# A slot table in DRAM in place of one-hot matmuls, and small tiles on 128 rows, in a routed expert layer

## The chip, the cores and the metric

The kernel runs on one core of one Trainium2 chip. The metric is the device time of one execution in microseconds (us). The median of three runs of the kernel before is 2848.63 us (2845.64 to 2850.64).

## The reference, cut to what matters

One encoder layer works on 1024 tokens of 1024 channels. After a mixing part (Fourier branch, attention, projections) comes a routed expert part, and that is what the change touches:

```
logits = u @ w_router + b_router                 # 1024 x 32
top_vals, top_idx = top_k(logits, 4)
top_w = softmax(top_vals)
for each expert e, for the tokens that chose it:
    h = u[tokens] @ w_gate_up[e] + b_gate_up[e]  # 1024 -> 2048
    gate = min(h[:, :1024], 7);  up = clip(h[:, 1024:], -7, 7)
    act = (up + 1) * gate * sigmoid(1.702 * gate)
    y = act @ w_down[e] + b_down[e]              # 1024 -> 1024
    out[tokens] += y * top_w
```

All of it is in 32-bit floats. Each product of matrices is made of three products of rounded halves (`hi` and `lo`), so each weight must be split on the chip into `whi` and `wlo` before TensorE may use it.

## The kernel before

**Routing.** The tokens go in eight tiles of 128. For tile `i`, `logits(i)` finds the four chosen experts, and `place(i)` counts with two small matmuls (L878, L879) which slot of each expert a token gets, and computes the weights (L889). The weights are cut into three bf16 parts (L897 to L900) and, with the slot numbers, transposed (L904) into `ct`. `accumulate(i)` multiplies `ct` with the expert biases `b_down` and adds the result to the output rows `acc_d` by an accumulating DMA on GpSimd's queue (L924, L926). At the end `in_order` (L932) turns slot numbers and weights into the order of the ranked experts (`posR`, `RH`). The experts are ranked by load after tile 6 (`ranking`); from there on rank 0 is the fullest.

**The expert stage.** Ranks 0 to 13 hold more than 128 slots and form lane a; ranks 14 to 31 hold 128 or 64 and form lane b. `plan` (from `moe_plan`) interleaves the two lanes step by step. An expert has twelve chunks of weights of 1 MB, so there are 384 chunks: steps 0 to 7 for gate and up, 8 to 11 for down; lane b has two more steps that transpose the activations (`at`, L1204). SyncE (SP) issues the loads of the chunks in the order of the plan, from three buffers `wraw` (`pew`, bufs=3). Per chunk ScalarE makes `whi` (L144) and VectorE `wlo` (L145); the chunk's buffer is free when both have read it.

**Tokens of an expert.** They are handled in 51 blocks of up to 128 slots, 33 in lane a and 18 in lane b. For a block, `one_hot` compares slot numbers with an iota on VectorE (L1080), eight bf16 matmuls with the one-hot tile (L1088) yield six numbers per slot, they are copied (`q6`, L1090), and `slot_info` makes from them the token for the gather (`gi`), the row for the scatter (`si`) and the weight (`wt`) in six short VectorE instructions (L997 to L1003). GpSimd gathers the rows of `u2_d` by an indirect DMA into `xya` or `xyb` (L1007); TensorE transposes them (L1103). In lane b, `rows` starts each pair of chunks with a matmul of the tile `sel` and the biases `b2`, both on 64 partitions (L1179), followed by the weights' own matmuls (L1183, L1184). `weigh` multiplies the result by `wt` (L1226 to L1230), and GpSimd adds it to `acc_d` by an indirect DMA, the scatter (L1011), once the fourth chunk of down is done. The next expert of a lane is fetched while the present one is at its chunks of gate and up.

A loop for experts that overflow their slots follows (from L1347); it has no rounds with this input.

Of the kernel before, what the change touches and what calls it, by code (L numbers as in the profile page):

```python
# [23 lines left out]
P = 128  # L24
# [6 lines left out]
NB_MAX = 64  # L31
ALPHA = 2.0 ** 0.25
# [63 lines left out]
def f32(ap):  # L96
    return ap.bitcast(F32)
# [7 lines left out]
def layer_kernel(ctx, tc, x, c, w_ada, b_ada, w_in, q_norm_g, k_norm_g, w_fourier, w_attn_o, w_out,  # L105
                 ln1_g, ln1_b, w_router, b_router, w_gate_up, b_gate_up, w_down, b_down,
                 ln2_g, ln2_b, t_cd, t_seq, t_rope, t_cap, t_idx, out):
# [5 lines left out]
    RS = "right"  # L113
# [104 lines left out]
    pyt = fo.enter_context(tc.tile_pool(name="pyt", bufs=1, side=RS))  # L218
# [3 lines left out]
    pfw = fws.enter_context(tc.tile_pool(name="pfw", bufs=1, side=RS))  # L222
# [29 lines left out]
    with tc.tile_pool(name="px", bufs=1) as px, tc.tile_pool(name="pada", bufs=3) as pada:  # L252
# [12 lines left out]
        act.dma_start(acc_d[S:S + P, :], x[0:P, :])  # L265
        xs = px.tile([P, NX, D], F32, name="xs")
# [70 lines left out]
    with tc.tile_pool(name="pfc", bufs=1) as pfc, tc.tile_pool(name="pf", bufs=2) as pf:  # L337
# [71 lines left out]
        pw1 = gws.enter_context(tc.tile_pool(name="pw1", bufs=2, side=RS))  # L409
# [260 lines left out]
    pm_ = ms_.enter_context(tc.tile_pool(name="pm", bufs=1, side=RS))  # L670
# [17 lines left out]
    pwo = ms_.enter_context(tc.tile_pool(name="pwo", bufs=2, side=RS))  # L688
# [26 lines left out]
    posR = route.tile([P, NX, NE], F32, name="posR")  # L715
    RH = route.tile([P, NX, NE, 6], BF16, name="RH")
    BG = route.tile([P, 16, NE], F32, name="BG")
    RB = route.tile([P, P], F32R, name="RB")
    R2 = route.tile([2 * NE, NE], F32R, name="R2")
    b2 = route.tile([2 * NE, 2048], F32R, name="b2")  # L720
# [5 lines left out]
    iota = route.tile([P, 448], F32, name="iota")  # L726
    pool.iota(iota, pattern=[[1, 448]], base=0, channel_multiplier=0, allow_small_or_imprecise_dtypes=True)
    iop = route.tile([P, 1], F32, name="iop")
    pool.iota(iop, pattern=[[0, 1]], base=0, channel_multiplier=1, allow_small_or_imprecise_dtypes=True)
    idx = route.tile([P, 2], F32, name="idx")  # L730
    sp.dma_start(idx, t_idx)
    dump = route.tile([P, 2], F32, name="dump")
    vec.tensor_scalar(dump[:, 0:1], iop, float(S), None, op0=ALU.add)
    vec.tensor_scalar(dump[:, 1:2], dump[:, 0:1], -1.0, None, op0=ALU.mult)
    with tc.tile_pool(name="pow", bufs=2) as pow_, tc.tile_pool(name="poc", bufs=1) as poc, ExitStack() as pos_, \
# [19 lines left out]

        for j in range(2):
# [4 lines left out]
            act.activation(b2[:, js], bgu[:2 * NE, :], AF.Copy)  # L761
            vec.tensor_tensor(b2[NE:, js], bgu[NE:2 * NE, :], f32(b2)[NE:, js], op=ALU.subtract)

        bdr = po_.tile([P, D], F32, name="xn", bufs=1)
        pool.memset(bdr[:NE, :], 0.0)
        for t in range(1, 4):
            act.dma_start(bdr[t * NE:(t + 1) * NE, :], b_down[0])
        vec.tensor_tensor(bdr, bdr, g2b, op=ALU.mult)
        bd = split(bdr, poc.tile([P, D], F32R, name="bdh"), poc.tile([P, D], F32R, name="bdl"))
# [13 lines left out]
        for i in range(NX):  # L783
            pool.memset(RH[:, i, :, 0], float(i))
        pool.tensor_copy(RH[:, :, :, 1], iop[:, :, None].to_broadcast([P, NX, NE]))
        pool.memset(RH[:, :, :, 2], 1.0)

# [86 lines left out]
        def place(i):  # L874
# [4 lines left out]
            pe_.matmul(ps[:, 32:64], oneb, before[:, i, :], start=False, stop=True)  # L879
            nm = po_.tile([P, 1], F32, name="nm")  # L880
# [8 lines left out]
            vec.tensor_scalar(e4, e4, sm, None, op0=ALU.mult)  # L889
            vec.tensor_tensor(oh4, oh4, e4[:, :, None].to_broadcast([P, TOPK, NE]), op=ALU.mult)  # L890
            wt = po_.tile([P, NE], F32, name="wt")
            vec.tensor_reduce(wt, oh4.rearrange("p k e -> p e k"), axis=AX.X, op=ALU.add)
            cat = po_.tile([P, 4, NE], F32, name="cat", bufs=1)
            part = po_.tile([P, NE], BF16, name="part")
            eng = vec if i >= NX - 2 else pool
            for t in range(3):
                eng.tensor_copy(part, wt)  # L897
                eng.tensor_copy(cat[:, 1 + t, :], part)
                if t < 2:
                    eng.tensor_tensor(wt, wt, cat[:, 1 + t, :], op=ALU.subtract)  # L900
            vec.tensor_tensor(cat[:, 0, :], ps[:, 32:64], mk, op=ALU.mult)
# [6 lines left out]
        def accumulate(i):  # L908
# [4 lines left out]
            for n in range(2):  # L913
# [3 lines left out]
                pe_.matmul(ab, ct[:, i, :], bd[0][:, ns], start=True, stop=False)  # L917
                pe_.matmul(ab, ct[:, i, :], bd[1][:, ns], start=False, stop=True)
# [8 lines left out]

        def in_order(h):

            pr = poh.tile([P, 4, 4, NE], F32, name="psh")  # L930
            for i in range(4):
                pe_.matmul(pr[:, i].rearrange("p t e -> p (t e)"), ct[:, 4 * h + i, :], RB, start=True, stop=True)  # L932
            vec.tensor_copy(posR[:, 4 * h:4 * h + 4], pr[:, :, 0, :])
            return pr

        def ranking(i):
# [13 lines left out]
            vec.tensor_scalar(R2, iota[:2 * NE, 0:NE], rank[:2 * NE], None, op0=ALU.is_equal)  # L950
            pe_.matmul(kp[0:1, 64:96], iop[:NE, :], f32(R2)[0:NE, :], start=True, stop=True)
            vec.tensor_copy(eidi, kp[0:1, 64:96])
            vec.tensor_tensor(rank, rank, idx[:, 1:2], op=ALU.add)
            vec.tensor_scalar(RB, iota[:, 0:P], rank, None, op0=ALU.is_equal)
# [24 lines left out]
        turn = place(NX - 1)  # L979
        halves = [in_order(0)]  # L980
        turn()
        halves.append(in_order(1))
        for h, pr in enumerate(halves):
            vec.tensor_copy(RH[:, 4 * h:4 * h + 4, :, 3:6], pr[:, :, 1:4, :].rearrange("p i t e -> p i e t"))
# [6 lines left out]
    def slot_info(pl, q6, m):  # L991

        tf = pl.tile([P, 2], F32, name="tf", bufs=4)
        gi = pl.tile([P, 1], I32, name="gi", bufs=10)
        si = pl.tile([P, 1], I32, name="si", bufs=10)
        wt = pl.tile([P, 1], F32, name="wt", bufs=10)
        vec.scalar_tensor_tensor(tf[:m, 0:1], q6[:m, 0:1], float(P), q6[:m, 1:2], op0=ALU.mult, op1=ALU.add)  # L997
        vec.tensor_copy(gi[:m], tf[:m, 0:1])

        vec.scalar_tensor_tensor(tf[:m, 1:2], q6[:m, 2:3], dump[:m, 1:2], tf[:m, 0:1], op0=ALU.mult, op1=ALU.add)  # L1000
        vec.tensor_scalar(tf[:m, 1:2], tf[:m, 1:2], dump[:m, 0:1], None, op0=ALU.add)
        vec.tensor_copy(si[:m], tf[:m, 1:2])
        vec.tensor_reduce(wt[:m], q6[:m, 3:6], axis=AX.X, op=ALU.add)  # L1003
        return gi, si, wt

    def gather(xg, gi, m):
        pool.indirect_dma_start(out=xg[:m, :], out_offset=None, in_=u2_d[0:S, :],  # L1007
                                in_offset=bass.IndirectOffsetOnAxis(ap=gi[:m, :], axis=0))

    def scatter(y, si, m):  # L1010
        pool.indirect_dma_start(out=acc_d, out_offset=bass.IndirectOffsetOnAxis(ap=si[:m, :], axis=0),  # L1011
                                in_=y[:m, :], in_offset=None, compute_op=ALU.add)
# [36 lines left out]
    with tc.tile_pool(name="pew", bufs=3, side=RS) as pew, tc.tile_pool(name="pes", bufs=1, side=RS) as pes, \  # L1049
# [5 lines left out]

        def chunk_loader(r, i, reg):
            def f():
                if i == 0:
                    reg["w"] = weights_of(sp.value_load(eidi[0:1, r:r + 1], min_val=0, max_val=NE - 1))
                return load_chunk(pew, *reg["w"], i, r >= N_BIG)  # L1060
            return f
# [7 lines left out]
        class Expert:  # L1069
# [7 lines left out]
            def one_hot(self, b):  # L1077
                b0, m = self.blocks[b][:2]
                self.hot[b] = pes.tile([P, NX, m], BF16, name="moh" + self.t, bufs=1)
                vec.tensor_tensor(self.hot[b], iota[:, None, b0 + 1:b0 + m + 1].to_broadcast([P, NX, m]),  # L1080
                                  posR[:, :, self.r:self.r + 1].to_broadcast([P, NX, m]), op=ALU.is_equal)

            def fetch(self, b):
                b0, m = self.blocks[b][:2]
                oh = self.hot.pop(b)
                pc = pep.tile([P, 512], F32, name="ptr", bufs=1)
                for i in range(NX):
# [22 lines left out]
            def start(self):  # L1110
# [3 lines left out]
                if self.t == "b":  # L1114
                    m = 2 * n if n in (32, 64) else n
                    self.m = m
                    self.sel = pe.tile([2 * NE, P], F32R, name="sel")
                    if m > n:
                        vec.tensor_scalar(self.sel[:, n:m], ones[:2 * NE, n:m], 0.0, None, op0=ALU.mult)
# [383 lines left out]
```

## Time and profile before

| | |
|---|---|
| median of three runs | 2848.63 us |
| the profiled execution | 2844.59 us, its span 2842.9 us |
| granted TensorE clock, mean | 0.954 of full speed |
| mixing part | up to about 905 us |
| routing of the tokens | 905 to 1045 us |
| from routing to the first expert matmul | 1045 to 1066 us |
| expert stage | 1066 to 2787 us |
| last additions and norm | 2787 to 2843 us |

Busy time over the span is 92% for TensorE (PE), 76% for VectorE (DVE), 50% for ScalarE (ACT) and 15% for GpSimd (POOL). The expert stage is three fifths of the span, so a saving there of one microsecond per block or per chunk counts tens or hundreds of times, while one in the routing counts eight times at most. "Issue" columns of SP (SPq) show when SP handed a load to the DMA queues, not when the data arrived.

### The profile page before, as it was taken

Reading aid. Unit: us, or ns where it says so; the run is one execution under the profiler, and the core shown is the slowest. Engines: PE = TensorE matmul, PEld = TensorE weight load, DVE = VectorE, ACT = ScalarE, POOL = GpSimd, SP = SyncE. Lnnn points to the kernel's source line nnn. Section 1 sums busy time; section 2 is a strip of 40 time slices with the busy share of each in tenths; the row PEclk is TensorE's granted clock in tenths of the full one; section 3 lists DMA queues with packets and bytes.
Section 4 is the critical chain, followed back from the end, with each engine's and each line's share of the span. In section 5 each row is a group of like instructions: output and inputs, shape, how many; then the busy total and the mean of one; then the engine's idle time right before and its main releaser. Section 6 shows DMA issues by size and latency. Waiting matters only on the chain. (4 is left out here: it accounts for less than half of the span.)

```text
span 2842.9 us, 44216 instructions
## 1 busy us (share of the span) xinstructions
PE 2609.5 (92%) x16380; PEld 2324.6 (82%) x16380; DVE 2160.1 (76%) x4047; ACT 1421.8 (50%) x2188; POOL 421.8 (15%) x316
## 2 busy tenths in 40 slices
PE   6999999899998958899999999998999999999991
PEld 5888899799888847699888888887988888888881
DVE  7543338777655878877898798979888888887885
ACT  3411122466622535645565556656655665665661
POOL 3100002111032530100201011011111010110003
PEclk9999999999999968899999999999999999999996
DMA  6154420000054467857988699877888888887774
GB/s 215 54 190 158 149 70 16 16 1 1 1 188 145 120 178 225 265 166 227 277 273 269 213 280 283 275 229 263 277 267 256 260 277 262 287 275 244 245 246 149
DMA packets 458747, 553.90 MB, mean 195 GB/s; under 512 B 18504, under 2 KB 396816, under 8 KB 458512
## 3 DMA queue, kind: packets, MB, share of 16 engines
q1 hardware_dynamic: 441632, 494.36, 53.4%
q0 software_dynamic: 15872, 53.12, 8.1%
q10 hardware_dynamic: 1024, 3.57, 0.4%
q8 instruction: 130, 2.13, 0.3%
q14 instruction: 89, 0.73, 0.1%
HBM read 505.54 MB, written 45.97 MB: 194 GB/s over the span
## 5 line engine op out<-in xcount | busy, mean ns | idle before, releaser
L145 DVE TENSOR_TENSOR wlo<-wraw,whi 128x1024 fp32r<-128x1024 f32 x768 | 914.6, 1220 | 184.7 <-ACT whi L144 179.0
L144 ACT ACTIVATE whi<-wraw 128x1024 fp32r<-128x1024 f32 x768 | 768.4, 1051 | 504.9 <-DMA wraw<-in_w_gate_up_dram 117.2
L1143 PE MATMUL psg<-xTa,wlo 128*128 128x160 f32 (+7 forms) x1792 | 476.0, 278 | 1.2 <-DVE wlo L145 1.2
L1143 PEld LDWEIGHTS psg<-xTa,wlo 128*128 128x128 f32 x1792 | 342.3, 194 | 4.4 <-DVE wlo L145 1.7
L1139 PE MATMUL psg<-xTa,whi 128*128 128x320 f32 (+3 forms) x1024 | 309.0, 368 | 14.9 <-DVE gu L1153 14.1
L138 PE MATMUL psd<-whi,aTa 128*128 128x256 f32 (+2 forms) x768 | 221.1, 292 | 21.5 <-ACT aTa L1167 14.1
L1141 PE MATMUL psg<-xTa,whi 128*128 128x256 f32 (+3 forms) x768 | 232.2, 307 | 3.3 <-ACT whi L144 3.3
L1142 PE MATMUL psg<-xTa,whi 128*128 128x256 f32 (+3 forms) x768 | 230.6, 303 | 0.0
L140 PE MATMUL psd<-whi,aTa 128*128 128x256 f32 (+2 forms) x768 | 218.1, 288 | 0.9 <-DVE aTa L1168 0.7
L139 PE MATMUL psd<-wlo,aTa 128*128 128x256 f32 (+2 forms) x768 | 217.6, 286 | 0.0
L1139 PEld LDWEIGHTS psg<-xTa,whi 128*128 128x128 f32 x1024 | 197.5, 195 | 24.1 <-issue 11.6
L138 PEld LDWEIGHTS psd<-whi,aTa 128*128 128x128 f32 (+2 forms) x768 | 146.1, 191 | 28.7 <-ACT aTa L1167 16.3
L1011 POOL DMA_INDIRECT acc_d<-xya,si x33 | 63.3, 1919 | 655.7 <-DVE xya L1230 523.9
L1183 PE MATMUL psr<-whi,xTb 128*128 128x512 f32 x352 | 155.1, 441 | 0.9 <-ACT whi L144 0.9
L1141 PEld LDWEIGHTS psg<-xTa,whi 128*128 128x128 f32 x768 | 145.0, 189 | 6.9 <-ACT whi L144 3.7
L1184 PE MATMUL psr<-wlo,xTb 128*128 128x512 f32 x352 | 149.5, 425 | 0.6 <-DVE wlo L145 0.6
L140 PEld LDWEIGHTS psd<-whi,aTa 128*128 128x128 f32 (+2 forms) x768 | 145.5, 191 | 2.5 <-DVE aTa L1168 1.4
L139 PEld LDWEIGHTS psd<-wlo,aTa 128*128 128x128 f32 (+2 forms) x768 | 146.3, 191 | 1.5 <-DVE wlo L145 0.2
L1142 PEld LDWEIGHTS psg<-xTa,whi 128*128 128x128 f32 x768 | 144.3, 188 | 1.6
L144 ACT ACTIVATE wh<-wraw 128x1024 fp32r<-128x1024 f32 (+1 forms) x35 | 48.0, 1376 | 152.1 <-PE psg L203 84.1
L149 ACT ACTIVATE pth<-pst 128x512 fp32r<-128x512 f32 x128 | 75.0, 598 | 86.5 <-PE pst L627 85.2
L138 PE MATMUL pz<-wh,uh 128*128 128x256 f32 x384 | 110.0, 286 | 2.4 <-DVE mrow L475 2.4
(488 smaller groups left out, 6602.0 us busy)
## 6 DMA issues: line engine op xcount, KB each, us to landing
wraw<-in_w_gate_up_dram SPq DMA_DIRECT2D x512, 512.0 KB
wraw<-in_w_down_dram SPq DMA_DIRECT2D x128, 1024.0 KB
wa<-in_w_ada_dram SPq DMA_DIRECT2D x24, 1024.0 KB
wraw<-in_w_in_dram SPq DMA_DIRECT2D x13, 1024.0 KB
xs<-in_x_dram SPq DMA_DIRECT2D x8, 512.0 KB
m_d<-sgm POOLq DMA_DIRECT2D x8, 512.0 KB, 5.3
sa_d<-sgm POOLq DMA_DIRECT2D x8, 512.0 KB, 2.9
wraw<-in_w_attn_o_dram SPq DMA_DIRECT2D x8, 512.0 KB
```

What stands on the lines that cost most here:

```text
L138: pe_.matmul(o, lh, rh, start=start, stop=False)
L139: pe_.matmul(o, lh, rl, start=False, stop=False)
L140: pe_.matmul(o, ll, rh, start=False, stop=stop)
L144: act.activation(hi, raw, AF.Copy)
L145: (lo_eng or vec).tensor_tensor(lo, raw, f32(hi), op=ALU.subtract)
L149: act.activation(hi, ps, AF.Copy)
L1139: pe_.matmul(ps[:, :2 * n], wh[:, k, cs], xT[:, 4 * h + k, :, :], start=first, stop=False)
L1141: pe_.matmul(ps[:, :n], wh[:, k, cs], xh, start=first, stop=False)
L1142: pe_.matmul(ps[:, :n], wh[:, k, cs], xl, start=False, stop=False)
L1143: pe_.matmul(ps[:, :n], wl[:, k, cs], xh, start=False, stop=last)
L1183: pe_.matmul(o, xk, wh[:, k, :], start=False, stop=False)
L1184: pe_.matmul(o, xk, wl[:, k, :], start=False, stop=last)
```

## The change

Now each token's number and weight are written by `place` straight to a table in DRAM, `slot_d`, one row of two words per slot of each expert. VectorE makes the row (`row`, `r4`, `rf`, `rowi`) and copies the weight into `vals`; GpSimd writes the rows with four indirect DMAs of 128 rows of 8 bytes per tile of tokens (`put`, 32 in all). Rows that nobody writes hold a dump row and weight zero from the input `t_slot`. `in_order`, `posR`, `RH` and `RB` are gone, and the bias product of `accumulate` is one matmul in place of two.

In the expert stage `one_hot`, its eight matmuls, `q6` and `slot_info` are gone. Per expert, `table` loads the expert's part of `slot_d` by one DMA on SP's queue into a tile `taba` or `tabb`, of which each lane has two. The column 0 of the table serves the gather and the scatter as index, the column 1 is the weight. The table of the lane's next expert is asked for at step 1 of the present one. Gathers always fetch 128 rows, transposes always take 128 rows, `sel` and `b2` have 128 partitions (the added ones zero), and GpSimd clears the lower half of the activations `xyb` of the experts with 64 slots.

```diff
+            row = po_.tile([P, NE], F32, name="row")
+            vec.tensor_tensor(row, ps[:, 32:64], eoff, op=ALU.add)
+            r4 = po_.tile([P, TOPK, NE], F32, name="r4")
+            vec.tensor_tensor(r4, oh4, row[:, None, :].to_broadcast([P, TOPK, NE]), op=ALU.mult)
+            rf = po_.tile([P, TOPK], F32, name="rf")
+            vec.tensor_reduce(rf, r4, axis=AX.X, op=ALU.add)
+            ri = po_.tile([P, TOPK], I32, name="rowi")
+            vec.tensor_copy(ri, rf)
...
+            vec.tensor_copy(f32(vals)[:, i, :, 1], e4)
+            for k in range(TOPK):
+                put = pool.indirect_dma_start(
+                    out=slot_d, out_offset=bass.IndirectOffsetOnAxis(ap=ri[:, k:k + 1], axis=0),
+                    in_=vals[:, i, k, :], in_offset=None)
...
-                pe_.matmul(ab, ct[:, i, :], bd[0][:, ns], start=True, stop=False)
-                pe_.matmul(ab, ct[:, i, :], bd[1][:, ns], start=False, stop=True)
+                pe_.matmul(ab, ct[:, i, :], bd[:, ns], start=True, stop=True)
...
-            def one_hot(self, b):
-                b0, m = self.blocks[b][:2]
-                self.hot[b] = pes.tile([P, NX, m], BF16, name="moh" + self.t, bufs=1)
...
+            def table(self):
+
+                nb = len(self.blocks)
+                e = expert_of(self.r)
+                tab = pes.tile([P, nb, 2], I32, name="tab" + self.t, bufs=2)
+                rows = slot_d.rearrange("(e r) c -> e r c", e=NE)[bass.ds(e, 1), 0:nb * P, :]
+                sp.dma_start(tab, rows.rearrange("o (b p) c -> p (o b) c", p=P))
+                for b in range(nb):
+                    self.blocks[b] += [tab[:, b, 0:1], f32(tab)[:, b, 1:2]]
 
             def fetch(self, b):
-                for i in range(NX):
-                    pe_.matmul(pc[:m, 0:6], oh[:, i, :], RH[:, i, self.r, :], start=i == 0, stop=i == NX - 1)
-                q6 = pes.tile([P, 6], F32, name="q6", bufs=4)
-                vec.tensor_copy(q6[:m], pc[:m, 0:6])
-                gi, si, wt = slot_info(pes, q6, m)
                 xg = PXY[self.t].tile([P, D], F32, name="xy" + self.t, bufs=XY[self.t])
-                gather(xg, gi, m)
-                self.blocks[b] += [si, wt, xg]
+                gather(xg, self.blocks[b][2])
+                self.blocks[b] += [xg]
...
-                    pe_.transpose(pt[:, j, :m], xg[:m, k * P:(k + 1) * P], ident[:m, :m])
+                    pe_.transpose(pt[:, j, :], xg[:, k * P:(k + 1) * P], ident)
...
-                    self.sel = pe.tile([2 * NE, P], F32R, name="sel")
+                    self.sel = pe.tile([P, P], F32R, name="sel")
...
                     self.av = pes.tile([P, D], F32, name="xyb", bufs=XY["b"])
+                    if n < P:
+                        pool.memset(self.av[n:, :], 0.0)
...
-                if 1 <= i <= nb_:
-                    nx.one_hot(i - 1)
+                if i == 1 and nx:
+                    nx.table()
```

Three places show how the instructions moved. The first is SP's queue before the first expert matmul; `wraw` is a chunk of weights and `u2_d` the tokens that the gathers read. Before, the first chunks stand ahead of the last write of tokens but one:

```order
L1059 TENSOR_LOAD eidi_7774 [waits DVE_49,Activation_49]
L1023 DMA wraw_9855<-in_w_gate_up_dram 128x4x256 [waits DMAHW4_49,PE_49]
L1023 DMA wraw_9855<-in_w_gate_up_dram 128x4x256
L1023 DMA wraw_9864<-in_w_gate_up_dram 128x4x256 [waits DMAHW6_49]
L1023 DMA wraw_9864<-in_w_gate_up_dram 128x4x256 [waits DMAHW7_49]
L853 DMA u2_d_76<-xn_9323 128x1024 [waits DMAHW0_49,Pool_49]
L823 DMA acc_d_77<-rr_9343 128x1024 [waits DMAHW1_49,DVE_49]
L1023 DMA wraw_9873<-in_w_gate_up_dram 128x4x256 [waits DMAHW2_49]
L1023 DMA wraw_9873<-in_w_gate_up_dram 128x4x256 [waits DMAHW3_49]
```

Now the tables of the first expert of each lane stand ahead of the first chunk, and the first of them waits for a transfer of GpSimd's queue, the last `put`:

```order
L1077 DMA tabb_9799<-slot_d_77 128x2 [waits DMAHW1_49,DMASW3_49,PE_49]
L1077 DMA taba_9812<-slot_d_77 128x2x2 [waits DMAHW2_49]
L1012 DMA wraw_9833<-in_w_gate_up_dram 128x4x256 [waits DMAHW3_49,PE_49]
L1012 DMA wraw_9833<-in_w_gate_up_dram 128x4x256 [waits DMAHW4_49]
L1012 DMA wraw_9842<-in_w_gate_up_dram 128x4x256 [waits DMAHW5_49]
L1012 DMA wraw_9842<-in_w_gate_up_dram 128x4x256 [waits DMAHW6_49]
L1012 DMA wraw_9851<-in_w_gate_up_dram 128x4x256 [waits DMAHW7_49]
L1012 DMA wraw_9851<-in_w_gate_up_dram 128x4x256 [waits DMAHW0_49]
```

All weights of the stage have moved behind the end of the routing.

The second place is GpSimd's queue at the end of the routing, after the last arithmetic on tokens. Before, it holds the accumulating transfers (L924, L926) and then the gathers:

```order
L924 DMA acc_d_77<-abt_9338 128x512 [waits DMASW2_49,Activation_49]
L924 DMA acc_d_77<-abt_9593 128x512 [waits DMAHW7_49,DMASW3_49,Activation_49]
L926 DMA acc_d_77<-rr_9673 128x1024 [waits DMAHW2_49,DMASW4_49,Activation_49]
L924 DMA acc_d_77<-abt_9599 128x512 [waits DMASW5_49,Activation_49]
L926 DMA acc_d_77<-rr_9723 128x1024 [waits DMAHW1_49,DMASW6_49,Activation_49]
L1007 DMA xyb_9779<-u2_d_76,gi_9770 64x1024 [waits DMAHW0_49,DMAHW4_49,DMASW7_49,DVE_49]
```

Now the puts of the last tiles stand among them (tiles 4 and 5 before this piece, with five short instructions behind each; tiles 6 and 7 in it):

```order
L943 DMA acc_d_78<-abt_9628 128x512 [waits DMAHW1_49,DMASW3_49,Activation_49]
L905 DMA slot_d_77<-vals_7878,rowi_9645 36864x2 [waits DMASW4_49,DVE_49]
L905 DMA slot_d_77<-vals_7878,rowi_9645 36864x2 [waits DMASW5_49]
L905 DMA slot_d_77<-vals_7878,rowi_9645 36864x2 [waits DMASW6_49]
L905 DMA slot_d_77<-vals_7878,rowi_9645 36864x2 [waits DMASW7_49]
L905 DMA slot_d_77<-vals_7878,rowi_9733 36864x2 [waits DMASW0_49,DVE_49]
L905 DMA slot_d_77<-vals_7878,rowi_9733 36864x2 [waits DMASW1_49]
L905 DMA slot_d_77<-vals_7878,rowi_9733 36864x2 [waits DMASW2_49]
L905 DMA slot_d_77<-vals_7878,rowi_9733 36864x2 [waits DMASW3_49]
L921 MEMSET cat_9750 128x32 [waits PE_49]
L943 DMA acc_d_78<-abt_9633 128x512 [waits DMASW4_49,Activation_49]
L945 DMA acc_d_78<-rr_9716 128x1024 [waits DMAHW4_49,DMASW5_49,Activation_49]
```

Eight puts have come ahead of the last accumulating transfers and of the first gather.

The third place is SP's queue in the expert stage, where lane b passes from its first expert to its second. Before, a chunk of down is followed by the next chunks of gate and up:

```order
L1027 DMA wraw_10979<-in_w_down_dram 128x8x256 [waits DMAHW7_49,DVE_49]
L1023 DMA wraw_10998<-in_w_gate_up_dram 128x4x256 [waits DMAHW1_49,DMAHW0_49,DVE_49]
L1023 DMA wraw_10998<-in_w_gate_up_dram 128x4x256
L1023 DMA wraw_11023<-in_w_gate_up_dram 128x4x256 [waits DMAHW3_49,DMAHW2_49,DVE_49]
L1023 DMA wraw_11023<-in_w_gate_up_dram 128x4x256
```

Now the table of the third expert stands between them. It takes the tile of the first expert's table, so it waits for a transfer of GpSimd's queue that reads that tile (DMASW7, the first expert's scatter):

```order
L1016 DMA wraw_10848<-in_w_down_dram 128x8x256 [waits DMAHW5_49,DVE_49]
L1077 DMA tabb_10874<-slot_d_77 128x2 [waits DMASW7_49,DMASW6_49,DVE_49]
L1012 DMA wraw_10876<-in_w_gate_up_dram 128x4x256 [waits DMAHW7_49,DMAHW6_49,Activation_49]
L1012 DMA wraw_10876<-in_w_gate_up_dram 128x4x256
L1012 DMA wraw_10901<-in_w_gate_up_dram 128x4x256 [waits DMAHW1_49,DMAHW0_49,DVE_49]
```

A wait for a scatter has come between two loads of weights; it recurs with every later expert of a lane.

## Rows read from the trace of the kernel before

**Rows 1.** Windows by stage: us, busy PE, PEld, DVE, ACT, POOL, clock, DMA share, GB/s.
```profile
905.00:1045.00 140.00, 115.82 (x847) 108.60 (x846) 119.87 (x369) 66.80 (x136) 62.71 (x78) 0.87 0.50 148
1045.00:1066.00 21.00, 7.14 (x53) 5.69 (x53) 11.49 (x63) 2.64 (x6) 3.17 (x4) 0.50 0.60 144
1066.00:2787.00 1721.00, 1628.19 (x10270) 1450.02 (x10270) 1452.64 (x2642) 1014.21 (x1516) 192.25 (x98) 0.97 0.81 254
```
**Rows 2.** Waits of PE in the expert stage: us, times, longest.
```profile
PE psr L1179 <- DVE si L1002: 6.3, 3, 2.3
PE psr L138 <- ACT whi L144: 5.8, 4, 3.5
```
**Rows 3.** PE timeline, lane b, start of a chunk pair: start, us, instruction.
```profile
1461.33 0.28 PE L140 MATMUL psd<-whi,aTa 128*128 128x256 f32 x1
1461.54 0.49 PE L1179 MATMUL psr<-b,sel 64*128 64x512 f32 x1
1461.97 0.51 PE L1183 MATMUL psr<-whi,xTb 128*128 128x512 f32 x1
1462.31 0.39 PE L1184 MATMUL psr<-wlo,xTb 128*128 128x512 f32 x1
1462.54 0.39 PE L1183 MATMUL psr<-whi,xTb 128*128 128x512 f32 x1
...
1472.80 0.50 PE L1183 MATMUL psr<-whi,xTb 128*128 128x512 f32 x1
```
**Rows 4.** PE timeline, one-hot matmuls between matmuls of lane b.
```profile
1549.58 0.40 PE L1183 MATMUL psr<-whi,xTb 128*128 128x512 f32 x1
1549.90 0.32 PE L1088 MATMUL ptr<-RH,mohb 128*64 128x6 bf16 x5
1550.15 0.50 PE L1184 MATMUL psr<-wlo,xTb 128*128 128x512 f32 x1
1550.49 0.39 PE L1183 MATMUL psr<-whi,xTb 128*128 128x512 f32 x1
```
**Rows 5.** All of line L1080: count, ns min/median/max, first and last start.
```profile
L1080 DVE TENSOR_TENSOR moha<-iota,posR x33: 405/1203/1227, 1043.8 to 2577.9; 128x1024 bf16<-128x1024 f32 x21, 128x256 bf16<-128x256 f32 x6, 128x512 bf16<-128x512 f32 x3, 128x640 bf16<-128x640 f32 x2
L1080 DVE TENSOR_TENSOR mohb<-iota,posR x18: 671/676/1221, 1043.2 to 2446.3; 128x512 bf16<-128x512 f32 x11, 128x1024 bf16<-128x1024 f32 x7
```
**Rows 6.** SP timeline, issues of weights: start, us of issuing.
```profile
1034.84 7.36 SPq L1023 DMA_DIRECT2D wraw<-in_w_gate_up_dram  x6
1458.31 4.41 SPq L1023 DMA_DIRECT2D wraw<-in_w_gate_up_dram  x4
1468.61 11.37 SPq L1023 DMA_DIRECT2D wraw<-in_w_gate_up_dram  x8
2253.22 4.09 SPq L1023 DMA_DIRECT2D wraw<-in_w_gate_up_dram  x4
```
**Rows 7.** POOL timeline, scatters of lane b at the same places.
```profile
1463.07 3.73 POOL L1011 DMA_INDIRECT acc_d<-xyb,si  x1 [60.50 <-DVE xyb L1228]
2250.41 1.60 POOL L1011 DMA_INDIRECT acc_d<-xyb,si  x1 [44.80 <-DVE xyb L1230]
```
**Rows 8.** DMA issues: count, KB, median us to landing.
```profile
sa_d<-sgm POOLq DMA_DIRECT2D x8, 512.0 KB, 2.9
acc_d<-abt POOLq DMA_DIRECT2D x12, 256.0 KB, 4.6
acc_d<-xyb,si POOLq DMA_INDIRECT x18, 8.1
```
**Rows 9.** DVE and POOL timelines, end of the routing.
```profile
1026.34 0.19 DVE L858 TENSOR_TENSOR lg<-psl,brb 128x32 f32<-128x32 f32 x1 [1.85 <-PE psl L856]
1037.17 0.86 POOL L924 DMA_DIRECT2D acc_d<-abt  x1 [7.70 <-ACT abt L923]
1044.40 0.84 POOL L926 DMA_DIRECT2D acc_d<-rr  x1 [0.54 <-DMA wraw<-in_w_gate_up_dram]
1054.89 1.02 POOL L1007 DMA_INDIRECT xya<-u_d,gi  x1 [7.07 <-DMA acc_d<-rr]
1056.21 0.91 POOL L1007 DMA_INDIRECT xya<-u_d,gi  x1 [0.30 <-issue]
```
**Rows 10.** PE timeline, first expert matmul.
```profile
1065.31 0.79 PE L1179 MATMUL psr<-b,sel 64*128 64x512 f32 x1 [0.31 <-DVE xTa L150]
```

More of the change, by code (lines that the diff above doesn't have):

```diff
@@ L31 @@
 NB_MAX = 64
+RS = S + P
 ALPHA = 2.0 ** 0.25
@@ L889, in place @@
             vec.tensor_scalar(e4, e4, sm, None, op0=ALU.mult)
+            vec.tensor_copy(f32(vals)[:, i, :, 1], e4)
+            for k in range(TOPK):
+                put = pool.indirect_dma_start(
+                    out=slot_d, out_offset=bass.IndirectOffsetOnAxis(ap=ri[:, k:k + 1], axis=0),
+                    in_=vals[:, i, k, :], in_offset=None)
+                tc.declare_no_dep(put.ins, group="slots", reason="rows of different tokens")
+                tc.add_to_no_dep_group("slots", put.ins)
             vec.tensor_tensor(oh4, oh4, e4[:, :, None].to_broadcast([P, TOPK, NE]), op=ALU.mult)
@@ L926, in accumulate @@
                 pool.dma_start(acc_d[i * P:(i + 1) * P, :], t, accum_op=ALU.add)
[L928 to L934, printed above, removed]
         def ranking(i):
@@ L978, in layer_kernel @@
                 accumulate(i - 1)
[L979 to L984, printed above, removed]
+        place(NX - 1)()
         accumulate(NX - 1)
@@ L989, in layer_kernel, with gather, scatter @@
     b2v = b2.rearrange("e (t f) -> e t f", t=2)
[L991 to L1011, printed above, removed]
+    def gather(xg, slot):
+        pool.indirect_dma_start(out=xg, out_offset=None, in_=u2_d,
+                                in_offset=bass.IndirectOffsetOnAxis(ap=slot, axis=0))
+    def scatter(y, slot, m):
+        pool.indirect_dma_start(out=acc_d, out_offset=bass.IndirectOffsetOnAxis(ap=slot[:m, :], axis=0),
                                 in_=y[:m, :], in_offset=None, compute_op=ALU.add)
@@ L1312, in layer_kernel @@
         for e in firsts:
+            e.table()
             for b in range(len(e.blocks)):
-                e.one_hot(b)
                 e.fetch(b)
@@ L1362, in layer_kernel @@
-            oh = pv.tile([P, NX, P], BF16, name="voh")
-            vec.tensor_tensor(oh, iota[:, None, 1:P + 1].to_broadcast([P, NX, P]),
-                              pos[:, :, None].to_broadcast([P, NX, P]), op=ALU.is_equal)
-            pc = pvp.tile([P, 512], F32, name="vpc", bufs=1)
-            pc = pc[:, 0:6 * NE]
-            for i in range(NX):
-                pe_.matmul(pc, oh[:, i, :], RH[:, i].rearrange("p r s -> p (r s)"), start=i == 0, stop=i == NX - 1)
-            t6 = pv.tile([P, 6, NE], F32, name="vt6")
@@ L1370, in layer_kernel @@
-            vec.tensor_tensor(t6, pc.rearrange("p (r s) -> p s r", s=6),
-                              sel[:, None, :].to_broadcast([P, 6, NE]), op=ALU.mult)
-            q6 = pv.tile([P, 6], F32, name="vq6")
-            vec.tensor_reduce(q6, t6, axis=AX.X, op=ALU.add)
-            gi, si, wt = slot_info(pv, q6, P)
+            row = sp.value_load(be[0:1, 1:2], min_val=0, max_val=NE * RS - P)
+            tab = pv.tile([P, 2], I32, name="vtab")
+            sp.dma_start(tab, slot_d[bass.ds(row, P), :])
@@ L1386, in columns @@
+            vec.tensor_tensor(rc, idx[:, 0:1], bl[:, 2:3], op=ALU.is_equal)
+            eb = pv.tile([P, P], F32R, name="veb")
+            vec.tensor_copy(eb, rc.to_broadcast([P, P]))
             def columns(src, name):
```

132 lines of the change are left out of this document (59 added, 73 removed).

## The prediction

> **What bounds the kernel now.** I read the windows by stage first. The expert stage is 1721 of the 2843 us, and in it TensorE is busy for 1628 us, 95%, VectorE for 1453 us, 84%, and the DMA engines have a share of 0.81 [rows 1]. TensorE sets the pace, but closely followed: 384 chunks in 1721 us are 4.48 us per chunk, and the waits of TensorE for a weight are short and few; 5.8 us in four waits is the largest line of that kind [rows 2]. Then I read SP's timeline against TensorE's, to see how far ahead the weights run. The reader is to see one chain. SP issues a chunk at 1458.31; at 1468.61 it issues the chunk three places later into the same buffer, so the first was loaded and split by then, 10.3 us after its issue [rows 6]; TensorE reads it first at 1472.80 [rows 3]. So this chunk is split 4.2 us before its use: the stream of weights has a cover of about one chunk, no more.
>
> **Less work on TensorE.** In rows 3 the matmuls of 512 columns on 128 rows start 0.23 us apart (1462.31 to 1462.54). Around L1179, which uses 64 rows, the gaps are 0.21 before it (the step of the 256-column matmuls before it is 0.12, worked out from their place in the same pair of chunks: half of 0.23), 0.43 for it and 0.34 for the one behind it. Against 0.12, 0.23 and 0.23 that is 0.09 + 0.20 + 0.11 = 0.40 us. The line runs 72 times: 29 us, if 128 rows cost 0.23 there. Transposes of 32 or 64 rows come in groups of four: by the blocks' sizes 20 blocks of two groups and 11 experts of lane b with two more each, 62 groups. They have the same kind of edge, and I take the one ahead of them alone, 62 x 0.09 = 6 us, since their own matmuls are short.
>
> The Trainium skill, in "TensorE: Matmul & The Clock Gate", section "Why this matters for your kernels", says that a single matmul on 32 rows takes as long as one on 128, the gain lying only in tiles that run at the same time. By it these 35 us would be nothing. The trace differs: 0.43 us from the 64-row start to the next, 0.23 for a 128-row one.
>
> The one-hot matmuls of a block: between 1549.58 and 1550.49 three ordinary steps of 0.23 would be 0.69 less one that isn't there, 0.46, and the stretch takes 0.91, so five of the eight cost 0.45 us [rows 4]. The remaining three stand in further gaps. Blocks of 128 rows have no such edge, so I take 0.36 us as the mean of the 51 blocks: 18 us. The wait for `si`, 6.3 us [rows 2], goes too. Sum 29 + 6 + 18 + 6 = 59; some of it comes back as waits for weights, so I take -55, between -25 (the 64-row price wrong or met by waits) and -75 (all, and shorter queues on VectorE).
>
> **Less on VectorE, more elsewhere.** `one_hot` is 33 instructions of up to 1.2 us and 18 of 0.68 to 1.2 [rows 5], near 50 us, and seven short ones per block go as well. VectorE is not the bound, so I cost this at nothing beyond the waits counted; TensorE's 95% hide it. The larger gathers bring 51 x 128 - 4944 = 1584 rows of 4 KB more (4944 is the sum of the experts' slots), 6.5 MB, against 254 GB/s in 1721 us [rows 1]: 1.5% more traffic, at nothing while the share is 0.81; uncovered it is 26 us. The clearing of 64 rows on GpSimd lies beside a queue that is busy 192 of 1721 us [rows 1].
>
> **The tables hold up the weights.** A table load stands in SP's queue between two chunks and waits until the scatter of the lane's expert before the last has landed, since a lane has two table tiles. Queued behind it are all further weights; after them wait ScalarE's and VectorE's splits and TensorE. Of the 32 tables 28 take a used tile, 16 in lane b and 12 in lane a. The scatter's time is in the trace. In the sample, the chunk that the table would stand ahead of is the one of 1458.31; the scatter is issued at 1463.07 [rows 7] and such scatters land 8.1 us later [rows 8]: 1471.2, so the chunk is held 12.9 us. Less its cover of 4.2 that is 8.7 us of waiting. At 2253.22 the scatter came earlier (2250.41): 2250.41 + 8.1 - 2253.22 = 5.3 us, less 4.2, 1.1 us. The mean of the two is 4.9; 16 times it is 78 us. In lane a the table mostly stands two to four chunks later behind its scatters, so I take the lower price, 12 x 1.1 = 13. From these 91 I take a third off, because a held stream leaves the DMA engines to the scatter, and the nearest plain transfers on that queue land in 2.9 and 4.6 us [rows 8]: +60. The bounds are 0 and 16 x 8.7 = 139.
>
> **From routing to the expert stage.** The last logits came at 1026.34, the last accumulating transfer was issued at 1044.40, its landing held the gather of lane a to 1054.89 [rows 9], and the first expert matmul started at 1065.31 [rows 10], 20.9 us behind that issue. Six chunks had then been issued, three of them by 1042.2 [rows 6]. Now 16 puts (tiles 4 to 7) follow the last logits on GpSimd; a put is an indirect DMA, and two of those stand 1.32 us apart [rows 9]: 21 us. Ten short instructions of about 0.25 us and three transfers of 0.86 [rows 9] add 5 us, and the first index needs about 3 us. The last put is thus issued near 1055 to 1056 and lands 2.9 to 4.6 us later, near 1060. The table follows, by about 1063 the first gather, then the last accumulating transfer near 1064, and 20.9 us behind it the first expert matmul: 1085, that is +20. The weights, issued from 1060, are three chunks in at most 13 us and don't end later. The lower bound is +8 (puts overlap the routing's waits), the upper +38: were the three chunks to come one behind the other at the 10.3 us of rows 6, the last would be split at 1091, and the eviction of the transposed tokens, which ScalarE now does behind it, with the matmul some 12 us later, as from the gather of 1054.89 to 1065.31 before.
>
> The skill's "DMA: Bandwidth & Descriptors", section "Anatomy of one DMA", puts the fixed cost of a transfer at about 2 us, most of it the receipt of the write. By it the put would land some 2 us sooner than taken here and the term be +18; no run here shows such a small write so far.
>
> Within the routing VectorE has five more short instructions per tile, and one less, about 1 us by eight tiles, and it is busy 120 of 140 us [rows 1]: 0 to 8, I take +3. Two further copies at the start, 0.8 MB, 0 to 3: +1.
>
> **Sum.** -55 + 60 + 20 + 3 + 1 = +29 us. Against the profiled execution of 2844.6 that is 2873.6; the median of the runs shown lies 4.0 above that execution, so 2877.6, forecast 2878.
>
> **Rivals.**
> Scatters land early. The place is the table load ahead of the second pair of chunks; if a scatter that has the queues to itself lands as the plain transfers do, within about 3 us, the chunk of 1458.31 is held 7.7 us, and alone in the queues its own load may be 3 to 4 us shorter than 10.3: nothing is felt. It decides from a mean wait of 31 / 28 = 1.1 us per table downwards (55 - 24 = 31). For it speaks the second sample, against it the median of 8.1. With 10 us left for the tables: -55 + 10 + 24 = -21, time 2828; with the lower bound of the passage 2815.
>
> The parts balance: tables cost 30, the rest as above: -1, time 2848.
>
> The 128-row tiles bring nothing: the gaps of rows 3 belong to the change of line and operand, and a 128-row matmul in the place of L1179 keeps them. This is what the rule of "TensorE: Matmul & The Clock Gate" in the Trainium skill, cited above, would make of this kernel. Then 35 us of the gain fall away: +64, time 2913; with the tables at their bound above 2940. The start-to-start gaps of rows 3 speak against it, yet they hold one instance of each change.
>
> **How the numbers follow.** The forecast's case, tables felt, has 0.55, with its own range 2857 to 2915; early scatters 0.27; balance 0.08; the costly case 0.10. A measurement of this kernel can tell about 0.2%, 5.7 us, from no change. So faster 0.27, same 0.08, slower 0.65. The range 2812 to 2935 leaves out the end of the early case (about 0.08), and the end of the costly one (about 0.1).
>
> **What will show it.** Right, if SP's waits show table loads that end with a scatter, if the issue of weights has holes of 8 to 13 us every twenty chunks with TensorE waiting for `whi` just behind them, if L1179's successor starts about 0.23 us after it, and if the first expert matmul starts near 1085. Wrong, if table loads wait under 5 us, if TensorE's waits for weights stay at the few microseconds of before, or if the last put is issued long before 1050.

## The result, and the profile after

The changed kernel takes 2995.8 us, median of four runs, against 2847.1 for the kernel before, also of four. The ratio is 1.051, 95% interval 1.048 to 1.055: 5% slower. One of the four runs took 5891.8 us, about twice the others (2985.6 to 2995.9), for a reason that no trace here shows; the ratio leaves it out. The direction was forecast, the time (2878, range to 2935) was not.

The profiled execution has a span of 2994.0 us, 151.1 more than before. Three borders split it: the first expert matmul, the last one of the stage, and the end. First the windows of the changed kernel, with the columns of [rows 1]; the second row is the expert stage.

```profile
1027.00:1111.40 84.40, 20.11 (x70) 13.06 (x70) 27.20 (x104) 16.22 (x27) 33.55 (x46) 0.50 0.53 138
1111.40:2939.20 1827.80, 1613.77 (x9896) 1451.46 (x9896) 1393.11 (x2260) 1015.91 (x1516) 170.49 (x107) 0.94 0.77 242
```

The stage now ends 1827.8 us after its first matmul. Before, from 1065.31 [rows 10] to its last matmul at 2787.5, it was 1722.2. So +105.6 us arose in the stage and +46.1 up to its first matmul, which starts at 1111.43; the tail is 0.6 shorter. TensorE has 376 matmuls fewer in the records and is busy only 15.6 us less than the 1629.4 that it was between these borders before. Its granted clock in the stage fell from 0.97 to 0.94, the share of the DMA engines to 0.77.

The waits say where the stage lost. First those of SP in it, then those of TensorE for split weights (us, times, longest):

```profile
SPq L1077 <- DMA acc_d<-xyb,tabb: 174.7, 16, 14.9
SPq L1077 <- DMA acc_d<-xya,taba: 173.3, 15, 21.3
```

```profile
PE psr L1175 <- ACT whi L147: 59.1, 16, 10.1
PE psr L141 <- ACT whi L147: 26.4, 11, 7.4
PE psg L1133 <- ACT whi L147: 17.5, 6, 6.4
PE psr L1176 <- DVE wlo L148: 13.3, 23, 0.8
```

SP stood 348 us at the table loads, waiting for scatters. TensorE waited 143.4 us for `whi` and `wlo` in all lines together; before it was 19.5 us, 5.8 us in the largest such line [rows 2].

One hold can be followed through four engines. The timelines of GpSimd, SP, ScalarE and TensorE in the changed kernel, start and duration in us, with the idle time before in brackets:

```profile
1509.50 3.72 POOL L1000 DMA_INDIRECT acc_d<-xyb,tabb  x1 [13.51 <-DVE xyb L1220]
```

```profile
1501.68 0.37 SPq L1016 DMA_DIRECT2D wraw<-in_w_down_dram  x1
1516.65 0.34 SPq L1077 DMA_DIRECT2D tabb<-slot_d  x1
1517.25 2.15 SPq L1012 DMA_DIRECT2D wraw<-in_w_gate_up_dram  x4
```

```profile
1522.31 2.00 ACT L147 ACTIVATE whi<-wraw 128x1024 fp32r<-128x1024 f32 x2 [5.61 <-DMA wraw<-in_w_gate_up_dram]
```

```profile
1518.26 0.40 PE L1171 MATMUL psr<-b,sel 128*128 128x512 f32 x1
1518.50 0.60 PE L1093 MATMUL ptr<-ident,xya 128*128 128x128 f32 x4
1523.42 0.80 PE L1175 MATMUL psr<-whi,xTb 128*128 128x512 f32 x1 [4.32 <-ACT whi L147]
...
1525.27 0.63 PE L1175 MATMUL psr<-whi,xTb 128*128 128x512 f32 x1
1525.70 0.63 PE L1176 MATMUL psr<-wlo,xTb 128*128 128x512 f32 x1
...
1529.84 0.51 PE L1176 MATMUL psr<-wlo,xTb 128*128 128x512 f32 x1 [0.76 <-DVE wlo L148]
1530.18 0.40 PE L1175 MATMUL psr<-whi,xTb 128*128 128x512 f32 x1
1530.42 0.40 PE L1176 MATMUL psr<-wlo,xTb 128*128 128x512 f32 x1
```

And two windows of the same stretch, with the columns of [rows 1]; the last but two is the granted clock:

```profile
1523.40:1528.50 5.10, 4.62 (x12) 3.24 (x12) 2.96 (x3) 2.43 (x4) 0.00 (x0) 0.52 1.06 368
1528.50:1533.00 4.50, 3.49 (x17) 2.24 (x16) 4.11 (x5) 3.73 (x6) 0.00 (x0) 1.00 1.03 318
```

The scatter is issued at 1509.50 and SP goes on at 1516.65, 7.1 us later. No chunk was issued from 1501.68 to 1517.25. ScalarE idles for the weights until 1522.31, TensorE for 4.32 us until 1523.42. And then its matmuls of 512 columns start 0.43 us apart (1525.27, 1525.70) in place of 0.24 (1530.18, 1530.42): the lower of its two clock levels, 1.2 in place of 2.4 GHz, for about five more us, in which the granted clock is 0.52. This hold is thus paid twice. The matmul with `sel` takes 0.24 us to its successor now (1518.26 to 1518.50), where the one with 64 rows took 0.43 [rows 3].

The end of the routing, where [rows 9, 10] stood: GpSimd's timeline of one tile of tokens (tile 4) and of the last put with what follows, VectorE's of the start of two tiles, ScalarE's of the two evictions of tile 4, and SP's behind the last put.

```profile
1040.60 1.07 POOL L905 DMA_INDIRECT slot_d<-vals,rowi  x1 [0.68 <-DVE rowi L892]
...
1044.59 0.97 POOL L905 DMA_INDIRECT slot_d<-vals,rowi  x1 [0.30 <-issue]
...
1046.36 0.12 POOL L921 MEMSET cat<- 128x32 f32 x1
...
1074.12 0.97 POOL L905 DMA_INDIRECT slot_d<-vals,rowi  x1 [0.31 <-issue]
...
1083.09 1.05 POOL L996 DMA_INDIRECT xyb<-u_d,tabb  x1 [6.03 <-DMA tabb<-slot_d]
...
1097.13 1.05 POOL L996 DMA_INDIRECT xyb<-u_d,tabb  x1 [11.11 <-DMA tabb<-slot_d]
1098.48 0.98 POOL L996 DMA_INDIRECT xya<-u_d,taba  x1 [0.30 <-issue]
```

```profile
1039.04 0.19 DVE L886 TENSOR_TENSOR row<-psb,eoff 128x32 f32<-128x32 f32 x1 [6.81 <-PE psb L884]
1046.98 0.29 DVE L925 CAST ct<-psb 128x128 fp32r<-128x128 f32 x1 [5.32 <-PE psb L924]
1053.80 0.19 DVE L886 TENSOR_TENSOR row<-psb,eoff 128x32 f32<-128x32 f32 x1 [6.52 <-PE psb L884]
```

```profile
1048.21 0.60 ACT L942 ACTIVATE abt<-psb 128x512 f32<-128x512 f32 x1 [7.71 <-PE psb L937]
1052.90 0.60 ACT L942 ACTIVATE abt<-psb 128x512 f32<-128x512 f32 x1 [4.09 <-DMA acc_d<-abt]
```

```profile
1076.53 0.37 SPq L1077 DMA_DIRECT2D tabb<-slot_d  x1
1077.10 0.39 SPq L1077 DMA_DIRECT2D taba<-slot_d  x1
1077.73 7.35 SPq L1012 DMA_DIRECT2D wraw<-in_w_gate_up_dram  x6
1085.27 4.55 SPq L1077 DMA_DIRECT2D tabb<-slot_d  x1
```

The puts of tile 4 run from 1040.60 to past 1045; only then does GpSimd make the parts `cat` of that tile, which end with the clearing at 1046.36. TensorE transposes them, `ct` follows at 1046.98, then the bias product in two halves, each evicted by ScalarE into the one tile `abt` (the second eviction, at 1052.90, waits for the first half's transfer to `acc_d`), and the one tile `psb` is free for the next tile's count: `row` of tile 5 at 1053.80, 14.8 us after that of tile 4. So the puts delay not only what reads the table but each following tile. The last put is issued at 1074.12. The first gather then waits 6.0 us for its table. The gathers of lane a stand behind a further gather of lane b whose table SP issued after three chunks of weights; it waits 11.1 us more.

### The profile page after: what moved, and what is told of

It reads as the page before. It is cut to its first block, busy times and chain, and to the rows that moved or that the text cites. A ratio compares the mean times of both kernels' runs of the same rounds, so it can differ in the third digit from the quotient of the medians.

```text
span 2994.0 us, 43077 instructions
## 1 busy us (share of the span) xinstructions
PE 2589.6 (86%) x15948; PEld 2321.0 (78%) x15948; DVE 2102.1 (70%) x3656; ACT 1423.8 (48%) x2188; POOL 431.2 (14%) x338
## 3 DMA queue, kind: packets, MB, share of 16 engines
q10 hardware_dynamic: 1088, 4.39, 0.4%
## 5 line engine op out<-in xcount | busy, mean ns | idle before, releaser
L1135 PE MATMUL psg<-xTa,wlo 128*128 128x160 f32 (+7 forms) x1792 | 469.7, 278 | 1.9 <-DVE wlo L148 1.6
L1176 PE MATMUL psr<-wlo,xTb 128*128 128x512 f32 x352 | 157.0, 446 | 13.4 <-DVE wlo L148 13.3
L1000 POOL DMA_INDIRECT acc_d<-xya,taba x33 | 66.2, 2006 | 591.5 <-DVE xya L1222 465.8
L143 PEld LDWEIGHTS psd<-whi,aTa 128*128 128x128 f32 (+2 forms) x768 | 143.4, 188 | 3.3 <-DVE aTa L1160 2.9
L1175 PEld LDWEIGHTS psr<-whi,xTb 128*128 128x128 f32 x352 | 74.6, 212 | 78.2 <-ACT whi L147 66.6
```

Source lines behind the costliest of these rows:

```text
L143: pe_.matmul(o, ll, rh, start=False, stop=stop)
L1135: pe_.matmul(ps[:, :n], wl[:, k, cs], xh, start=False, stop=last)
L1175: pe_.matmul(o, xk, wh[:, k, :], start=False, stop=False)
L1176: pe_.matmul(o, xk, wl[:, k, :], start=False, stop=last)
```

## The experiments

"Stage" is the time from the first expert matmul to the end of the last one in the profiled execution. In the changed kernel it is 1827.8 us and begins at 1111.4; before, 1722.2 and 1065.3.

**Four table tiles (e1).**

```diff
-                tab = pes.tile([P, nb, 2], I32, name="tab" + self.t, bufs=2)
+                tab = pes.tile([P, nb, 2], I32, name="tab" + self.t, bufs=4)
```

> The changed kernel with four table tiles per lane in place of two, so that a table load finds a tile whose scatters landed long ago. Theory (table loads hold SP's queue): the 348 us that SP waited at the table loads for scatters nearly vanish, TensorE's waits for whi and wlo fall from about 140 to about 20 us, the expert stage from 1828 to 1670-1700 us, the whole to 2845-2870 us. Rival (the larger gathers and the tables' own traffic slow the stream of weights): the stage stays above 1790 us, the whole above 2955 us.

Measured: 2834.8 us, ratio to the kernel before 0.995 (0.993 to 0.997); the stage 1679.8 us; of SP's waits for scatters at the table loads 0.4 us are left; TensorE's waits for weights fall to 41.3 us, not to the 20 of the theory. Windows of the stage, first of this run, then of the one with small tiles (e3, below):

```profile
1108.80:2788.60 1679.80, 1570.60 (x9896) 1438.07 (x9896) 1388.25 (x2259) 1013.55 (x1516) 172.63 (x107) 0.97 0.83 263
```

```profile
1112.30:2809.30 1697.00, 1604.15 (x9896) 1430.78 (x9896) 1389.49 (x2262) 1013.19 (x1516) 156.69 (x97) 0.97 0.82 261
```

Nothing but the number of tiles differs from the changed kernel, and 148.0 us of the stage are gone. Of these, 43.2 are busy time: 9896 matmuls took 1613.8 us there and 1570.6 here, with the clock at 0.94 and 0.97. The other 104.8 are idle time. These are single executions, and the profiled one of e1 was the slowest of its seven runs (2845.2 us); the six other kernels below whose holds are gone or nearly gone have stages of 1671 to 1686 us, by which the 148 would lie between 142 and 157. The rival fell: the gathers are as large here as there, and the stream moves 263 GB/s.

**The table loads on GpSimd's queue (e2).**

```diff
-                e = expert_of(self.r)
+                e = pool.value_load(eidi[0:1, self.r:self.r + 1], min_val=0, max_val=NE - 1)
-                sp.dma_start(tab, rows.rearrange("o (b p) c -> p (o b) c", p=P))
+                pool.dma_start(tab, rows.rearrange("o (b p) c -> p (o b) c", p=P))
```

> The changed kernel, two table tiles, with the table loads issued from GpSimd's queue in place of SP's. Theory (it is the in-order queue of SP that matters, not the wait itself): the wait for the scatter now holds only GpSimd, the expert stage is 1670-1720 us. Rival (a late table makes the gather and the transposes late, whoever issues it): the stage stays above 1780 us. The routing may be longer, since GpSimd loads the expert numbers into its registers there.

Measured in one run: 2834.8 us, the stage 1672.7. GpSimd's waits at the table loads:

```profile
POOL tabb L1077 <- DMA acc_d<-xyb,tabb: 95.0, 16, 8.3
POOL taba L1077 <- DMA acc_d<-xya,taba: 63.4, 11, 7.2
```

Still two tiles, and the scatter is still waited for, but on a queue that carries no weights. So it is the queue, not the wait, that costs.

**The table asked for later (e9).**

```diff
-                if i == 1 and nx:
+                if i == 3 and nx:
...
-                if 2 <= i < nb_ + 2:
-                    nx.fetch(i - 2)
+                if 4 <= i < nb_ + 4:
+                    nx.fetch(i - 4)
```

> The changed kernel with its two table tiles, but the next expert's table asked for at step 3 in place of step 1, and its blocks fetched from step 4 in place of step 2. Theory (the hold is a matter of place in SP's queue: how long before the scatter's landing the load stands): the load stands two chunks of its lane later, some three to four chunks of the plan or 13 to 17 us; most holds of lane b (up to 15 us) vanish, those of lane a (up to 21 us) shrink, the stage is 1690 to 1745 us, the whole 2855 to 2910 us. Rival (whatever its place, a load that reuses a tile holds the stream, or late gathers cost as much): the stage stays above 1790 us.

Measured: 2843.9 us, ratio 1.000 (0.998 to 1.001); the stage 1676.1. SP's waits at the table loads in this run:

```profile
SPq L1077 <- DMA acc_d<-xya,taba: 36.3, 8, 14.5
SPq L1077 <- DMA acc_d<-xyb,tabb: 28.4, 9, 7.3
```

Of 348 us of holds 65 are left, and the profiled stage is as short as with four tiles, better than the theory's 1690 to 1745. So two steps remove most of the cost in the same two tiles. The whole doesn't show all of it gone: the ratio lies above e1's 0.995, and the intervals don't touch.

**Four tiles in lane b only (e6), three in both (e7).**

```diff
-                tab = pes.tile([P, nb, 2], I32, name="tab" + self.t, bufs=2)
+                tab = pes.tile([P, nb, 2], I32, name="tab" + self.t, bufs=4 if self.t == "b" else 2)   # e6
+                tab = pes.tile([P, nb, 2], I32, name="tab" + self.t, bufs=3)                           # e7
```

> The changed kernel with four table tiles in lane b and two in lane a. The scatters that held SP were 16 of lane b (175 us of waiting) and 15 entries of lane a (173 us). Theory (each lane's waits cost about what they hold SP): the stage of 1828 us loses about half of the 148 us that four tiles in both lanes took away, 1745 to 1765 us. Rival (lane a's waits are covered, as the prediction had it, 13 us): 1700 us or less.

Measured in one run: 2907.3 us, the stage 1740.1, just under the theory's range. Its window:

```profile
1111.40:2851.50 1740.10, 1585.08 (x9896) 1440.24 (x9896) 1389.83 (x2260) 1015.12 (x1516) 158.31 (x107) 0.96 0.80 254
```

So lane b's holds cost 1827.8 - 1740.1 = 87.7 us and, once these are gone, lane a's 1740.1 - 1679.8 = 60.3 more. In idle time of TensorE alone (the window less its busy time: 214.0 us in the changed kernel, 155.0 here, 109.2 in e1) it is 59.0 for lane b and 45.8 for lane a. The rival, my price of 13 us for lane a, fell.

> The changed kernel with three table tiles per lane. Theory (a tile is free when its scatter landed, one expert of the lane earlier than with two): as with four, a stage of 1675 to 1690 us and no waits of SP for scatters. Rival (the hold is some other wait of the table load, for a gather or a weight reading the tile): over 1720 us.

Measured in one run: 2844.7 us, the stage 1675.5, no wait for a scatter. In the stage, three tiles do as well as four; on the whole time, 1.002 of the kernel before beside it (2840.0), one run decides nothing.

**Small tiles undone (e3).** On e1; the transposes of the activations (`av`) change in the same way as those shown, and the clearing goes.

```diff
-                    pe_.transpose(pt[:, j, :], xg[:, k * P:(k + 1) * P], ident)
+                    pe_.transpose(pt[:, j, :m], xg[:m, k * P:(k + 1) * P], ident[:m, :m])
...
-                    pe_.matmul(o, self.sel[:, :m], b2v[:, :, c * 256:(c + 1) * 256], start=True, stop=False)
+                    pe_.matmul(o, self.sel[:2 * NE, :m], b2v[:2 * NE, :, c * 256:(c + 1) * 256], start=True, stop=False)
```

> Four table tiles, and the small tiles undone: transposes of as many rows as the block has, and the bias matmul on 64 partitions again (no clearing of the activations). Theory (a 64-row tile costs TensorE 0.40 us more at the bias matmul and 0.09 at a group of transposes): 20 to 35 us slower than the run with four table tiles alone. Rival (128 rows bring nothing): within 6 us of it.

Measured: 2867.9 us against e1's 2834.8, 33 us slower; the intervals of their ratios to the kernel before, 1.004 to 1.010 and 0.993 to 0.997, don't touch. The windows above show the same 9896 matmuls busy 1604.2 us here and 1570.6 in e1: 33.6 us, at the same clock of 0.97. Of that the profiled stage kept 17 us; the idle time shrank by the rest, 16 us, and TensorE's waits for weights are 25.8 us where e1 has 41.3. The profiled executions are 20 us apart, the medians 33, so how much comes through in the end is known only roughly. "TensorE: Matmul & The Clock Gate" of the Trainium skill, section "Why this matters for your kernels", has a lone matmul on few rows cost as much as one on 128; here, among matmuls on 128 rows, it costs more (0.43 us to its successor [rows 3], 0.24 with 128 rows), and the measurement decides.

**The routing: parts on VectorE (e4), weights first (e5), products on VectorE (e8).** Each on top of the one before, e4 on e1.

```diff
-            eng = vec if i >= NX - 2 else pool
+            eng = vec
-            pool.memset(cat[:, 3, :], 0.0)
+            eng.memset(cat[:, 3, :], 0.0)
```

> Four table tiles, and the parts of the weights (cat, with its clearing) made on VectorE for every tile of tokens, so that the transposition of a tile no longer waits behind the puts on GpSimd. Theory (the routing's chain runs through GpSimd: puts, then cat, then transposition, bias product and the next tile): the first expert matmul moves from 1111 to 1080-1095 us, the whole 15 to 30 us below the run with four table tiles alone. Rival (the 21 us of the last sixteen puts are the path themselves): the first expert matmul stays at 1105 or later.

Measured: 2827.3 us, ratio 0.993 (0.990 to 0.995). The first expert matmul starts at 1089.8 where e1's starts at 1108.8: 19 us. That is beyond the scatter of single executions: in the seven kernels that keep the chain it starts between 1105.7 and 1112.9, in the three without it between 1082.3 and 1089.8. Of the theory's 15 to 30 us for the whole the medians show 7.5, with intervals that overlap, the profiled executions 20. GpSimd's and SP's timelines of e4:

```profile
1057.23 0.97 POOL L905 DMA_INDIRECT slot_d<-vals,rowi  x1 [0.30 <-issue]
```

```profile
1063.65 0.36 SPq L1077 DMA_DIRECT2D tabb<-slot_d  x1
```

The last put is issued at 1057.23, 17 us sooner than in the changed kernel, and the first expert matmul starts 32.6 us behind it (37.3 there). That `cat` stood behind the puts on GpSimd was the cause of that part.

For e5, `wst.ahead(3)`, with the two waits that it had, moves ahead of the loop that asks for the first tables.

> As the run with four table tiles and cat on VectorE (e4), and the first three chunks of weights asked for ahead of the first two tables, as the kernel before had them. Theory (the first matmul waits for tables and for weights queued behind them, both behind the last put): the first expert matmul moves from 1090 to 1075-1085 us, the whole falls by 5 to 15 us. Rival (the puts and the gathers behind them set it alone, and the three splits now delay VectorE's last tiles, as they did before by 8 us): 1088 us or later, no gain.

Measured: 2814.9 us, ratio 0.991 (0.989 to 0.994), the lowest median of all. But no gain over e4 is shown. The medians are 12 us apart, but the kernel before took 2850.7 us beside e4 and 2840.0 beside e5, and the intervals of the two ratios overlap. In the profile the first expert matmul starts at 1088.8, 1 us sooner than in e4, and the last put comes at 1061.9, later. The stage is 1670.9 against e4's 1678.9, within the spread of stages named below. The rival, 1088 us or later and no gain, was right.

```diff
-            pool.tensor_tensor(xn, xn, sc2b, op=ALU.mult)
-            pool.tensor_tensor(xn, xn, sh2b, op=ALU.add)
+            e_ = vec if i == NX - 1 else pool
+            e_.tensor_tensor(xn, xn, sc2b, op=ALU.mult)
+            e_.tensor_tensor(xn, xn, sh2b, op=ALU.add)
```

> As e5, and the two products per element of the last tile of tokens (L856, L857) on VectorE in place of GpSimd, where they stood between the last puts, 2.35 us each. Theory (GpSimd's queue is the path at the end of the routing): the first expert matmul comes 3 to 5 us earlier than in e5. Rival (VectorE's own chain is the path there): the same or later.

Measured: 2821.6 us, ratio 0.994 (0.991 to 0.996). The first expert matmul comes at 1082.3, 6.5 us sooner than in e5, somewhat more than the theory's 3 to 5, but the stage is 1685.5, 14.6 longer, and the whole is no faster. The stages without holds lie between 1671 and 1686 us in seven kernels; what sets a kernel's place in that span was not tested.

## Why the prediction was wrong

The measured parts add up in the span of the profiled execution: -42.4 (e1's stage against the stage before) + 148.0 (holds) + 46.1 (up to the first matmul) - 0.6 (tail) = +151.1. The sum had -55 + 60 + 23 (the passage and the routing) + 1 = +29. So 88 us of the miss lie in the tables, 23 in the passage, 13 in the gain on TensorE.

- **What bounds the kernel.** Right. A stream of weights with a cover of one chunk does not bear a pause: SP's holds came out in TensorE's waits for `whi`.
- **Less work on TensorE, -55.** Near. The busy time fell by 58.8 us (1629.4 to 1570.6 in e1), against 53 in the parts that are matmuls (29 + 6 + 18; the last 6 of the 59 are a wait); the small tiles gave 33.6 of it, where 35 were reckoned. But only 42.4 came out: the idle time rose from 92.8 to 109.2, more than the 4 us that the forecast gave back. In e1 the waits for weights rose from 19.5 to 41.3; e2 and e9 have about as much idle time with waits of 23.5 and 18.8, so the weights are not the whole reason. The rival by which 128 rows bring nothing is refuted by e3.
- **The tables, +60. This is the step that failed, in its size.** The mechanism is shown by e1, e2 and e9; the term measured 148, above the bound of 139. Two parts of the pricing were wrong. First, lane a was taken as mostly covered, 13 us; it costs 60 (e6). Its 12 tables on used tiles held SP for 173.3 us, 14.4 each, longer than lane b's 16 with 174.7, 10.9 each. Four times a hold of lane b follows one of lane a two chunks later (1411.41 and 1427.35 in SP's timeline), which a price of single holds, each with its own cover, leaves out. Second, the clock was left out: 43.2 us of the 148 are more busy time for the same matmuls. Not all of that is the clock, since a matmul that follows a wait is also recorded as longer (0.51 us at 1529.84, 0.40 at 1530.18). An estimate of the clock's part is 30 us: in the stretches at the lower level TensorE was busy for 158 us in the changed kernel and for 98 in e1, and half of the difference is lost. The rest of the pricing was near: in idle time lane b cost 59.0 us (e6), where 78 less a third is 52, while lane a cost 45.8, where 13 less a third is 9. The third stood for scatters that land sooner in a held stream, 31 us over 28 tables; in the hold shown the scatter landed after 7.1 us in place of the 8.1 before [rows 8], which over 28 tables would be 28 us.
- **From routing to the stage, +20, and +3 within the routing.** It measured +46.1. The puts' own time was right, 1.27 to 1.38 us apart (1.32 taken). Their landing was taken as 2.9 to 4.6 us; SP went on 2.4 us behind the last put in the changed kernel (1074.12, 1076.53) and 6.4 in e4 (1057.23, 1063.65). And e4, with the last put at 1057 where 1055 to 1056 was forecast, starts at +24.5. The step that failed is that the puts were only added up on GpSimd behind the last logits: the `cat` casts were counted as 0.25 us each, not as links of a chain that goes, for each tile of tokens, through GpSimd, TensorE, VectorE, ScalarE and one PSUM tile. Its link on GpSimd cost 19 us (e4).
- **Rivals.** Early scatters: refuted; the rival had them land within about 3 us, the one shown took 7.1, and SP's mean wait per table was 12.4 us (348 / 28). Balance: refuted; the tables cost 148 us, not 30. Only with the holds gone does the kernel come near the one before, 0.995 (e1) to 1.000 (e9).
- **The signs named.** SP's table loads that end with a scatter, holes in the issue of weights (15.6 us in the one shown, where 8 to 13 were named) and the 0.24 us behind the `sel` matmul were all there. The first matmul was expected at 1085 and came at 1111.

The Trainium skill has the rule that was at work in the holds: "DMA: Bandwidth & Descriptors", section "Anatomy of one DMA", says that a DMA's semaphore wait is done by the issuing sequencer before it hands the transfer on. The section is on transfers that GpSimd issues; the trace agrees for SP's queue too, 348 us of SP's waits at L1077, and e2 shows what follows for the transfers queued behind.

## What to carry to other kernels

Before a small load goes into the queue that streams the weights, look up what it waits for, above all when it reuses a tile: a pause beyond the stream's cover comes out as idle time of the engine that needs the weights, and then once more in its clock. More tiles, a later request or a quieter queue each took most or all of the cost away, with one to three lines each. Price each lane or stream from its own rows; a lane that was only assumed to be covered was the largest single error in idle time here. When an engine's queue gets work added, follow what stands behind that work to the next stage's buffers, not just the added time.

## What the runs showed of the hardware

A wait of TensorE of 4.32 us was followed by about 5 us of matmuls at the lower clock level; over the stage the granted clock is 0.94 with the holds and 0.97 without (e1), and the same 9896 matmuls take 43.2 us more busy time with them. A load of 1 KB from a table in DRAM (128 rows of 8 bytes), issued at 1076.53 just ahead of 3 MB of weights, released its gather at 1083.09, 6.6 us later; what held it was not tested. An indirect write of 128 rows of 8 bytes takes GpSimd 0.97 us and its neighbour starts 1.27 us later.
